# Log-sum-exp over heads on one core: 4 MB block loads, and an earlier, direct crossing from whole tiles to half tiles

## The chip, the cores and the metric

The kernel runs on one core of one Trainium2 chip. The time is the device time of one execution in microseconds (us), and the median of several is quoted. A profile of one execution of each kernel was taken as well; its span is 1.7 to 2.2 us shorter than the device time of the same execution.

Names of the engines in the profile: PE is the matrix engine (PEld its weight loads), DVE the vector engine, ACT the scalar engine, POOL the GpSimd engine, SP the engine that here only issues transfers.

## The reference

```python
B, S, D, H = 8, 2048, 2048, 8          # float32; x is 134.2 MB
x_heads = x.reshape(B, S, H, Dh).transpose(0, 2, 1, 3)     # Dh = 256
x_heads = x_heads + bias[None, :, None, :]
x_tiled = np.repeat(x_heads, 2, axis=2)
lse = log(sum(exp(x_tiled), axis=-1))  # the maximum is taken out and put back
```

For each row and each of its 8 heads, one number comes out: the logarithm of the sum of 256 exponentials of x plus bias. Every result is written twice. The work is a stream: each of 134.2 MB is read once, and only 1 MB is written.

## The kernel before

x is worked off as 64 tiles of 256 rows (2 MB, two rows for each of 128 partitions). All four engines share a tile: PE adds the bias to the first three heads, ACT takes exponentials, POOL adds the bias to the last four heads, DVE multiplies head 3 by the exponential of its bias and adds up. Near the end, tiles are worked off in smaller pieces, so that less is left to do when the last byte lands.

```python
K = 2
NBUF = 9
BULK = dict(pe=3, acc=1, g0=4, late=True, fold=0)
MIXED = dict(pe=1, acc=1, g0=4, late=False, fold=0)
PROMPT_F1 = dict(pe=2, acc=2, g0=8, late=False, fold=1)
...
STAGES = [                       # first tile of a stage, its pieces
    (0, (BULK,)),                # whole tiles
    (54, (MIXED,)),              # whole tiles, less for PE
    (57, (PROMPT_F1, PROMPT_F1)),# half tiles (1 MB), two pieces
    (62, (SINGLE_F1, SINGLE_F1)),
    (63, (PROMPT_F2, TRIPLE)),
]
...
    T_PROMPT = STAGES[1][0]      # 54
```

A stage with two entries cuts its tiles into two pieces, `k0 = 0` and `k0 = 1`. A piece starts with its column `c0 = 0`.

```python
    for t in range(T):
        ...
        for k0, k1, c0, c1 in pieces(t):
            m = modes_of(t)[k0]
            ...
            if c0 == 0:
                if next_units and not m["late"]:
                    bias_there = put_bias(*next_units.pop(0))   # PE: bias of the next unit
                if t > T_PROMPT and m["g0"] == H:
                    keep_warm()                                 # PE: 3 matmuls without use
                if m["g0"] < H:
                    add = g_add(m, t, k0, k1)                   # POOL
                if t < T - 1 or k0 == 0:
                    flush(for_pool)          # ACT and DVE part of the unit before
            if t == T_PROMPT and c0 == 0:    # the first factors
                spread(one_ps, V0, W0)                                     # PE
                nc.scalar.activation(out=one_ps, in_=one_ps, func=ACT.Exp) # ACT
            ...
            for_pool.append(pool_part)       # later: exponential, reduction, next load
```

A "unit" is a whole tile or a half tile, worked off as one. `for_pool` holds back what needs POOL's addition: the exponential and the reduction of a whole tile are put into the queues one unit later. The "factors" are the exponentials of the bias of heads 1 and 2; from the small pieces on, DVE multiplies by them. Up to there their place in PSUM, `one_ps`, belongs to the PE part of whole tiles, which is why they are made at the crossing between the stages.

The softmax here doesn't subtract the row's maximum and nothing guards it: scores larger than these inputs give would overflow.

## Time and profile before

| | before |
|---|---|
| time, median of 3 | 326.7 us |
| profiled span | 325.4 us |
| loads | 57 of 2 MB, 12 of 1 MB, then smaller ones |
| busy share of DVE, POOL, ACT, PE | 87%, 89%, 81%, 81% |
| DMA | full in nearly every slice |

The prediction below shows the rows that tell what bounds the kernel. In the order of time, columns are start (us from the span's start), duration, engine, line, operation, operands and, in brackets, the engine's idle time just before and what ended it. At the crossing of before (tiles 53 and 54), and for the second half of tile 62:

```profile
274.37 2.34 ACT L331 ACTIVATE xt<-xt 128x2560 f32<-128x2560 f32 x1 [0.70 <-POOL xt L325]
277.05 0.58 ACT L500 ACTIVATE one_ps<-one_ps 128x512 f32<-128x512 f32 x1 [0.35 <-PE one_ps L182]
...
314.65 1.70 ACT L331 ACTIVATE xt<-xt 128x1792 f32<-128x1792 f32 x1
```

The first row is the exponential of tile 53, which had been held back. The second makes the factors, once, after a wait of 0.35 us for PE. The third will serve as a marker and is called the marker row below: it is the last exponential before the last tile, and from its start to the end of the span 10.75 us pass.

In the order of time of SP, the store of the first seven batches stands behind the last of the loads, so its start tells when the last loads were issued (SP waits there for earlier loads, 49.5 us in 18 waits over the whole of before, so it keeps pace with the DMA):

```profile
315.36 0.72 SPq L425 DMA_DIRECT2D out_dram<-res  x1
```

### The profile page before, as it was taken

The page shows a single profiled execution, that of the slowest core. Times are in us where ns is not written, and L with a number is a line of the kernel's source. Part 1 is how long each engine was busy: PE and PEld are TensorE (multiplying, and loading weights), DVE is VectorE, ACT ScalarE, POOL GpSimd, SP SyncE. Part 2 cuts the span into 40 slices and gives each one's busy share as a digit, 9 for nine tenths or more (in the row PEclk, how much of TensorE's full clock was granted, in tenths as well). Part 3 has the DMA queues.
Part 4 walks back from the last instruction along what each step waited for, and adds up shares of the span by engine and source line. Part 5 has one row for each costly group of instructions (what it writes and reads, how often), then busy time and mean ns, then how long its engine had stood idle before and what let it go on. Part 6 is the DMA issues. An engine that isn't in the chain of part 4 may idle for free.

```text
span 325.4 us, 2350 instructions
## 1 busy us (share of the span) xinstructions
PE 263.2 (81%) x649; PEld 98.6 (30%) x649; DVE 284.0 (87%) x306; ACT 264.7 (81%) x425; POOL 290.7 (89%) x123
## 2 busy tenths in 40 slices
PE   5398999599888789779779788887877897399984
PEld 2033333233323223223223223323223332044442
DVE  1008999999999999998998899989899799999985
ACT  1139999499969878987887969698788778889995
POOL 7999999899999999999999999999999899958874
PEclk9999999899979987997997979798998989569999
DMA  7999999999999999999999999999999999999995
GB/s 293 428 435 429 427 433 422 425 433 429 427 427 431 425 424 433 425 425 434 426 425 431 431 422 427 429 429 427 431 427 426 429 425 429 415 421 421 424 394 154
DMA packets 11934, 135.42 MB, mean 416 GB/s; under 512 B 1361, under 2 KB 1745, under 8 KB 2961
## 3 DMA queue, kind: packets, MB, share of 16 engines
q1 hardware_dynamic: 11824, 135.27, 98.9%
q8 instruction: 5, 0.08, 0.1%
q14 instruction: 7, 0.06, 0.0%
q0 software_dynamic: 96, 0.00, 0.0%
q10 hardware_dynamic: 2, 0.01, 0.0%
HBM read 134.23 MB, written 1.05 MB: 416 GB/s over the span
## 4 chain that ended last, share of the span: by engine, by line
DMA 48%; DVE 35%; POOL 6%; ACT 6%; PE 3%; issue 1%; SPq 0%; DVEq 0%
DMA xt<-in_x_dram 45%; DVE R L350 29%; ACT xt L331 5%; DVE xt L343 5%; POOL xt L325 4%; DMA b<-bparts 2%; PE pair L275 2%; DVE xt L366 2%; PE one_ps L275 1%; ACT xt L293 1%; DMA brow<-in_bias_dram 1%; POOL brest L173 1%; POOL brest L175 1%; PE pair L216 0%; POOL bparts L172 0%
## 5 line engine op out<-in xcount | busy, mean ns | idle before, releaser
L325 POOL TENSOR_TENSOR xt<-xt,b_rep 128x2048 f32<-128x2048 f32 x57 | 258.8, 4543 | 20.1 <-DMA xt<-in_x_dram 20.1
L350 DVE TENSOR_REDUCE R<-xt 128x14 f32<-128x3584 f32 (+1 forms) x56 | 214.5, 3831 | 1.9
L331 ACT ACTIVATE xt<-xt 128x2560 f32<-128x2560 f32 (+5 forms) x77 | 158.1, 2062 | 13.4 <-POOL xt L325 12.5
L275 PE MATMUL pair<-xt,ident 128*128 128x512 f32 x216 | 115.1, 660 | 0.0
L275 PE MATMUL one_ps<-xt,ident 128*128 128x512 f32 x108 | 66.7, 702 | 23.1 <-DMA xt<-in_x_dram 23.1
L293 ACT ACTIVATE xt<-pair 128x1024 f32<-128x1024 f32 x54 | 56.3, 1042 | 20.7 <-PE pair L275 19.3
L275 PEld LDWEIGHTS pair<-xt,ident 128*128 128x128 f32 x216 | 46.2, 214 | 61.5 <-issue 61.5
L343 DVE TENSOR_TENSOR xt<-xt,w_ps 128x512 f32<-128x512 f32 x54 | 36.8, 681 | 27.8 <-ACT xt L331 27.7
L286 ACT ACTIVATE xt<-one_ps 128x256 f32<-128x256 f32 x108 | 40.6, 391 | 7.9 <-PE one_ps L275 7.9
L216 PE MATMUL one_ps<-b,ones 3*128 3x512 bf16 x54 | 20.7, 383 | 18.4 <-ACT xt L286 12.4
L216 PEld LDWEIGHTS <-ones 3*128 3x128 bf16 x162 | 13.5, 92 | 70.2 <-issue 63.8
L216 PE MATMUL pair<-b,ones 3*128 3x512 bf16 x108 | 32.3, 378 | 0.0
L275 PEld LDWEIGHTS one_ps<-xt,ident 128*128 128x128 f32 x108 | 17.0, 198 | 46.4 <-DMA xt<-in_x_dram 39.6
L251 PE MATMUL pair<-xt,ident 128*128 128x512 f32 (+1 forms) x36 | 21.0, 669 | 7.2 <-DMA xt<-in_x_dram 7.1
L286 ACT ACTIVATION_READ_ACCUMULATOR xt<-one_ps 128x1 f32 x108 | 23.5, 218 | 0.0
L366 DVE CUSTOM_DVE_ANT_0 xt<-xt,w_ps 128x256 f32<-128x256 f32 x61 | 22.4, 419 | 0.0
L390 POOL TENSOR_TENSOR xt<-xt 128x128 f32<-128x128 f32 (+3 forms) x39 | 13.9, 356 | 3.1
L382 POOL TENSOR_TENSOR xt<-xt,w_sb 128x256 f32<-128x256 f32 (+1 forms) x13 | 10.1, 773 | 5.4 <-ACT xt L331 4.8
L266 PE MATMUL tpair<-ident 128*128 128x128 f32 x84 | 13.6, 300 | 0.5 <-ACT res L421 0.5
L306 ACT ACTIVATE xt<-pair 128x256 f32<-128x256 f32 x33 | 12.3, 387 | 0.0
L266 PEld LDWEIGHTS tpair<-ident 128*128 128x128 f32 x84 | 11.1, 200 | 4.1 <-issue 3.0
L366 DVE CUSTOM_DVE_ANT_0 xt<-xt,one_ps 128x256 f32<-128x256 f32 x27 | 10.6, 416 | 0.7 <-ACT xt L331 0.7
(40 smaller groups left out, 68.5 us busy)
## 6 DMA issues: line engine op xcount, KB each, us to landing
xt<-in_x_dram SPq DMA_DIRECT2D x57, 2048.0 KB, 30.8
xt<-in_x_dram SPq DMA_DIRECT2D x12, 1024.0 KB, 24.7
xt<-in_x_dram SPq DMA_DIRECT2D x4, 256.0 KB, 11.4
out_dram<-res SPq DMA_DIRECT2D x1, 896.0 KB, 6.6
xt<-in_x_dram SPq DMA_DIRECT2D x2, 384.0 KB, 16.0
xt<-in_x_dram SPq DMA_DIRECT2D x2, 128.0 KB, 6.3
out_dram<-res_last SPq DMA_DIRECT2D x1, 128.0 KB, 1.7
b<-bparts POOLq DMA_DIRECT2D x3, 1.5 KB, 6.4
```

The costliest lines, as they stand in the source:

```text
L216: nc.tensor.matmul(p, lhsT=ones3, rhs=each_row(b3, h * Dh, Dh, K), start=True, stop=False,)
L251: mm = nc.tensor.matmul(p, lhsT=ident, rhs=xts[t % NBUF][:, ka:kb, c : c + w], start=False, stop=True,)
L266: nc.tensor.matmul(tps[B % 2][:, 0], lhsT=ident, rhs=ident, start=True, stop=True)
L275: mm = nc.tensor.matmul(p, lhsT=ident, rhs=xts[t % NBUF][:, :, h * Dh : (h + 1) * Dh], start=False, stop=True,)
L286: act = nc.scalar.activation(out=xts[t % NBUF][:, k, 0:Dh], in_=got[0][:, k * Dh : (k + 1) * Dh], func=ACT.Exp, accum_out=sums[:, k, 0:1],)
L293: act = nc.scalar.activation(out=xts[t % NBUF][:, :, Dh : m["pe"] * Dh].rearrange("p k (h j) -> p h k j", j=Dh), in_=got[-1].rearrange("p ...
L325: add = nc.gpsimd.tensor_tensor(out=v, in0=v, in1=each_row(b_rep, c - G0, D - c, k1 - k0), op=ALU.add)
L331: return on_x(t, nc.scalar.activation(out=v, in_=v, func=ACT.Exp), [after])
L343: mul = nc.vector.tensor_tensor(out=f, in0=f, in1=each_row(w_ps, m["pe"] * Dh - W0, n, k1 - k0), op=ALU.mult,)
L350: red = nc.vector.tensor_reduce(out=sums[:, k0:k1, h0:H], in_=v.rearrange("p k (h j) -> p k h j", j=Dh), op=ALU.add, axis=mybir.AxisListTy ...
L366: ttr = nc.vector.tensor_tensor_reduce(out=v, in0=v, in1=w, scale=1.0, scalar=0.0, op0=ALU.mult, op1=ALU.add, accum_out=dst,)
L390: done = nc.gpsimd.tensor_tensor(out=v[:, :, 0:n], in0=v[:, :, 0:n], in1=v[:, :, n : 2 * n], op=ALU.add)
```

## The change

The intent: larger loads have fewer packets (the profile counts 11934 in before) and fewer ends, so a kernel that waits for bytes gets them sooner. Tiles 2 to 49 are loaded in pairs of 4 MB, the buffers (8 instead of 9) are freed in pairs, the mixed stage goes, and half tiles begin at tile 52 instead of 57. Warm matmuls go into the bank that the next unit will fill, and other preparations move.

```diff
 K = 2
-NBUF = 9
+KB = 4
+BLOCKS = 50
+NBUF = 8
+NEARLY = 5
...
 STAGES = [
     (0, (BULK,)),
-    (54, (MIXED,)),
-    (57, (PROMPT_F1, PROMPT_F1)),
+    (52, (PROMPT_F1, PROMPT_F1)),
     (62, (SINGLE_F1, SINGLE_F1)),
...
     def load(t):
+        if TB <= t < BLOCKS:
+            if t % TB == 0:
+                ...                      # waits for the last uses of both tiles of the buffer
+                    nc.sync.dma_start(
+                        out=xbs[t // TB % len(xbs)], in_=rows_of(t, TB)
+                    ),
+                ...
+            return
...
+                for _ in range(NWARM):   # in put_bias, outside the whole tiles
+                    mm = nc.tensor.matmul(
+                        p[:, 0:P], lhsT=ident, rhs=ident, start=True, stop=True
+                    )
...
-                if t > T_PROMPT and m["g0"] == H:
-                    keep_warm()
                 if m["g0"] < H:
                     add = g_add(m, t, k0, k1)
-                if t < T - 1 or k0 == 0:
+                if t != T_PROMPT and (t < T - 1 or k0 == 0):
                     flush(for_pool)
             if t == T_PROMPT and c0 == 0:
-                spread(one_ps, V0, W0)
-                nc.scalar.activation(out=one_ps, in_=one_ps, func=ACT.Exp)
+                first_factors()
```

Cut: the bias of the first five units goes to PE in three parts directly, the small transfers of the bias are issued by ACT instead of POOL, the other factors are made at tile 32, the sums and the transposes of a batch are laid out for four rows of a partition, and loads are issued from a list of their own. `T_PROMPT` is still the first tile of the second stage, now 52.

More of the change, by code (lines that the diff above doesn't have):

```diff
@@ L16 @@
 K = 2
-NBUF = 9
+KB = 4
+BLOCKS = 50
+NBUF = 8
+NEARLY = 5
 NWARM = 3
 BULK = dict(pe=3, acc=1, g0=4, late=True, fold=0)
-MIXED = dict(pe=1, acc=1, g0=4, late=False, fold=0)
 PROMPT_F1 = dict(pe=2, acc=2, g0=8, late=False, fold=1)
@@ L60 @@
     H, Dh = bias.shape
-    assert D == H * Dh and S % (P * K) == 0
+    assert D == H * Dh and S % (P * KB) == 0
     NBLK = S // (P * K)
+    NB = S // (P * KB)
+    TB = KB // K
     T = B * NBLK
     T_PROMPT = STAGES[1][0]
+    T_FACTORS = T // 2
     CPE = BULK["pe"] * Dh
@@ L84 @@
     brest = sb.tile([1, 2, CPE], F32, name="brest")
-    R = [sb.tile([P, K, H, NBLK], F32, name=f"R{b}") for b in range(B - 1)]
+    R = [sb.tile([P, KB, H, NB], F32, name=f"R{b}") for b in range(B - 1)]
     R_last = sb.tile([P, H, NBLK, K], F32, name="R_last")
-    res = sb.tile([H * NBLK, B - 1, P, K, 2], F32, name="res")
+    res = sb.tile([H * NB, B - 1, P, KB, 2], F32, name="res")
     res_last = sb.tile([P, P, 2], F32, name="res_last")
-    xts = [sb.tile([P, K, D], F32, name=f"xt{i}") for i in range(NBUF)]
+    xbs = [sb.tile([P, KB, D], F32, name=f"xb{i}") for i in range(NBUF // TB)]
+    xts = [xb[:, k : k + K] for xb in xbs for k in range(0, KB, K)]
     w_ps = pp.tile([P, W2 - W0], F32, name="w_ps")
@@ L96 @@
     ps = [p[:, c : c + MM] for p in pairs for c in (0, MM)]
-    tpair = pp.tile([P, 2, K, P], F32, name="tpair")
-    tps = [tpair[:, i] for i in range(2)]
+    tp = pp.tile([P, KB, P], F32, name="tp")
     def modes_of(t):
@@ L108, in pieces, with rows_of @@
         return [(k, k + 1, c0, c1) for k in range(K) for c0, c1 in cols[k]]
-    def rows_of(t):
-        b, blk = divmod(t, NBLK)
-        v = x[b, blk * P * K : (blk + 1) * P * K, :]
+    def rows_of(t, n=1):
+        b, at = divmod(t, NBLK)
         if b < B - 1:
-            return v.rearrange("(p k) d -> p k d", k=K)
+            blk, i = divmod(at, TB)
+            v = x[b, blk * P * KB : (blk + 1) * P * KB, :]
+            return v.rearrange("(p k) d -> p k d", k=KB)[:, i * K : (i + n) * K]
+        v = x[b, at * P * K : (at + 1) * P * K, :]
         return v.rearrange("(k p) d -> p k d", k=K)
-    users = [[] for _ in range(T)]
+    users = [[] for _ in xbs]
     def on_x(t, ins, after):
-        known = [u for u in users[t] if u.ins.engine != ins.ins.engine]
-        for before in range(t % NBUF, t, NBUF):
-            known += users[before]
-        for u in known:
-            if u not in after:
+        buf = users[t // TB % len(xbs)]
+        for t_u, u in buf:
+            same = u.ins.engine == ins.ins.engine
+            if u not in after and (not same or t_u % NBUF == t % NBUF and t_u < t):
                 tc.declare_no_dep(
-                    ins.ins, u.ins, reason="waited for by those it waits for"
+                    ins.ins,
+                    u.ins,
+                    reason="another tile, or waited for by those it waits for",
                 )
-        users[t].append(ins)
+        buf.append((t, ins))
         return ins
@@ L138, in load @@
     def load(t):
+        if TB <= t < BLOCKS:
+            if t % TB == 0:
+                after = [u for i in range(TB) if t >= NBUF for u in last_uses[t + i - NBUF]]
+                ins = on_x(
+                    t,
+                    nc.sync.dma_start(
+                        out=xbs[t // TB % len(xbs)], in_=rows_of(t, TB)
+                    ),
+                    after,
+                )
+                for i in range(TB):
+                    loads[t + i, 0, 0] = ins
+            return
         after = last_uses[t - NBUF] if t >= NBUF else []
@@ L148, in load, with reload @@
             )
+    def reload(t):
+        n = t + NBUF
+        if n < BLOCKS:
+            if n % TB == TB - 1:
+                load(n - TB + 1)
+        elif n < T:
+            load(n)
     order = tc.manual_schedule()
@@ L177 @@
     for i in range(3):
-        nc.gpsimd.dma_start(out=b3[i : i + 1, :], in_=bparts[:, i])
+        nc.scalar.dma_start(out=b3[i : i + 1, :], in_=bparts[:, i])
     def spread(dst, c0, c1):
@@ L188, with first_factors, other_factors @@
         nc.vector.tensor_copy(b_rep[:, c - G0 : c - G0 + MM], ps[i])
-    for c in range(W0, W2, MM):
-        spread(w_ps[:, c - W0 : c - W0 + MM], c, c + MM)
-    nc.scalar.activation(out=w_ps, in_=w_ps, func=ACT.Exp)
-    nc.scalar.activation(out=w_sb, in_=b_rep[:, W1 - G0 :], func=ACT.Exp)
+    w_late = w_ps[:, 0 : G0 - W0]
+    spread(w_late, W0, G0)
+    nc.scalar.activation(out=w_late, in_=w_late, func=ACT.Exp)
+    def first_factors():
+        spread(one_ps, V0, W0)
+        nc.scalar.activation(out=one_ps, in_=one_ps, func=ACT.Exp)
+    def other_factors():
+        nc.scalar.activation(
+            out=w_ps[:, G0 - W0 :], in_=b_rep[:, 0 : W2 - G0], func=ACT.Exp
+        )
+        nc.scalar.activation(out=w_sb, in_=b_rep[:, W1 - G0 :], func=ACT.Exp)
     n_ps = [0]
@@ L214, in put_bias @@
             got = [one_ps, pair[:, 0:MM], pair[:, MM : 2 * MM]]
+            parts = [(ones3, b3)]
+            if n_ps[0] <= NEARLY:
+                parts = [(ones3[0:1], bparts[:, i]) for i in range(3)]
             for h, p in enumerate(got):
-                nc.tensor.matmul(
-                    p,
-                    lhsT=ones3,
-                    rhs=each_row(b3, h * Dh, Dh, K),
-                    start=True,
-                    stop=False,
-                )
+                for i, (lhsT, b) in enumerate(parts):
+                    nc.tensor.matmul(
+                        p,
+                        lhsT=lhsT,
+                        rhs=each_row(b, h * Dh, Dh, K),
+                        start=i == 0,
+                        stop=False,
+                    )
             return got + [pair]
@@ L232, in put_bias @@
                 n_ps[0] += 1
+                for _ in range(NWARM):
+                    mm = nc.tensor.matmul(
+                        p[:, 0:P], lhsT=ident, rhs=ident, start=True, stop=True
+                    )
+                    on_bank(bank, mm)
                 mm = nc.tensor.matmul(
@@ L262, in add_x @@
         return heads
-    def keep_warm():
-        for _ in range(NWARM):
-            nc.tensor.matmul(
-                tps[B % 2][:, 0], lhsT=ident, rhs=ident, start=True, stop=True
-            )
     def late_heads(m, t, got, sums):
@@ L401, in add_up @@
             )
-            on_x(t, red, [done])
+            last_uses[t].append(on_x(t, red, [done]))
         return add_up
     def finish(b):
-        nr = H * NBLK
-        tp = tps[b % 2]
-        for k in range(K):
+        nr = H * NB
+        for k in range(KB):
             nc.tensor.transpose(
@@ L418, in finish @@
             offset=tp.offset,
-            ap=[[tp.ap[0][0], nr], [1, P], [P, K], [0, 2]],
+            ap=[[tp.ap[0][0], nr], [1, P], [P, KB], [0, 2]],
         )
@@ L425, in store @@
         nc.sync.dma_start(
-            out=out[0 : B - 1].rearrange("b h (n r) -> (h n) b r", n=NBLK),
+            out=out[0 : B - 1].rearrange("b h (n r) -> (h n) b r", n=NB),
             in_=res.rearrange("q b p k r -> q b (p k r)"),
@@ L430, in finish_last @@
     def finish_last():
-        tp = tps[(B - 1) % 2][:, 0]
+        last = tp[:, KB - 1]
         nc.tensor.transpose(
-            out=tp, in_=R_last.rearrange("p h n k -> p (h n k)"), identity=ident
+            out=last, in_=R_last.rearrange("p h n k -> p (h n k)"), identity=ident
         )
         tv = bass.AP(
-            tensor=tp.tensor, offset=tp.offset, ap=[tp.ap[0], [1, P], [0, 2]]
+            tensor=last.tensor, offset=last.offset, ap=[last.ap[0], [1, P], [0, 2]]
         )
@@ L448, in sums_of @@
         if b < B - 1:
-            return R[b][:, :, :, blk]
+            return R[b][:, blk % TB * K :, :, blk // TB]
         return R_last[:, :, blk, :].rearrange("p h k -> p k h")
@@ L455 @@
     for_pe = []
+    for_load = []
     next_units = [
@@ L471 @@
     for t in range(T):
+        if t == T_FACTORS:
+            other_factors()
         xt = xts[t % NBUF]
@@ L511 @@
                 flush(for_pe)
+                flush(for_load)
             if not m["late"]:
@@ L525, in pool_part @@
                     later(m, t, k0, k1, sums, add)
-                if k1 == K and t + NBUF < T:
-                    load(t + NBUF)
+                if k1 == K:
+                    for_load.append(lambda: reload(t))
             for_pool.append(pool_part)
```

## The prediction

> **What bounds the kernel now.** I read the page's 40 slices first, then busy time by stretch, then the DMA view in two windows, then single engines in order of time.
>
> From the page:
>
> ```profile
> DMA  7999999999999999999999999999999999999995
> GB/s 293 428 435 429 427 433 422 425 433 429 427 427 431 425 424 433 425 425 434 426 425 431 431 422 427 429 429 427 431 427 426 429 425 429 415 421 421 424 394 154
> ```
>
> The 16 DMA engines are full from the second slice to the one before the last. Every compute engine has more idle time than that (DVE 87%, POOL 89%, ACT 81% busy). So in the bulk the kernel waits for bytes: its time is the start before the first packet, the time that the packets need, and what is left to do after the last one. The chain of waits agrees with 45% on the loads; where it names DVE, from 26 to 121 us, DVE works off a late start with full buffers behind it and the DMA is as full as later.
>
> Busy time by stretch (columns: window, length, busy time per engine, clock, DMA share, GB/s):
>
> ```profile
> 180.00:260.00 80.00, 65.92 (x152) 23.30 (x151) 74.02 (x34) 67.02 (x103) 73.36 (x18) 0.91 1.01 428
> 280.00:290.00 10.00, 7.65 (x11) 1.75 (x11) 10.00 (x28) 8.54 (x13) 8.68 (x2) 0.50 1.01 422
> 290.00:300.00 10.00, 9.51 (x45) 5.50 (x45) 10.00 (x49) 10.00 (x19) 6.56 (x15) 0.96 1.01 420
> ```
>
> Full in all three, but 428 GB/s with 2 MB loads and 420 with 1 MB loads. The DMA view of a window of each kind shows what differs (230 to 260 us, then 290 to 310 us):
>
> ```profile
> DMA packets 879, 12.82 MB, mean 427 GB/s; under 512 B 96, under 2 KB 96, under 8 KB 96
> ...
> q8 instruction: 1, 0.02, 0.2%
> q14 instruction: 1, 0.01, 0.1%
> ```
>
> ```profile
> DMA packets 1156, 8.41 MB, mean 421 GB/s; under 512 B 129, under 2 KB 129, under 8 KB 129
> ```
>
> Without the tiny ones: 783 packets for 12.82 MB, 16.4 KB each, which is two 8 KB rows, what one partition gets from a 2 MB load. In the later window 1027 packets for 8.41 MB, 8.2 KB, one row. The tiny ones are some 16 to a load. So each engine moves 8 large packets and a tiny one per load, and the large one is as long as the contiguous run of a partition.
>
> The price of a packet comes from arrivals. POOL's addition starts when its tile has landed (it waited about 0.35 us for the DMA each time), and so does PE in the half units:
>
> ```profile
> 185.90 4.54 POOL L325 TENSOR_TENSOR xt<-xt,b_rep 128x2048 f32<-128x2048 f32 x1 [0.34 <-DMA xt<-in_x_dram]
> ...
> 249.54 4.55 POOL L325 TENSOR_TENSOR xt<-xt,b_rep 128x2048 f32<-128x2048 f32 x1 [0.35 <-DMA xt<-in_x_dram]
> 255.10 4.54 POOL L325 TENSOR_TENSOR xt<-xt,b_rep 128x2048 f32<-128x2048 f32 x1 [1.02 <-DMA xt<-in_x_dram]
> ...
> 279.59 4.55 POOL L325 TENSOR_TENSOR xt<-xt,b_rep 128x2048 f32<-128x2048 f32 x1 [0.38 <-DMA xt<-in_x_dram]
> 284.55 4.54 POOL L325 TENSOR_TENSOR xt<-xt,b_rep 128x2048 f32<-128x2048 f32 x1 [0.41 <-DMA xt<-in_x_dram]
> ```
>
> ```profile
> 304.64 1.13 PE L251 MATMUL pair<-xt,ident 128*128 128x512 f32 x2 [0.19 <-DMA xt<-in_x_dram]
> ...
> 312.11 0.70 PE L251 MATMUL pair<-xt,ident 128*128 128x256 f32 x2 [0.29 <-DMA xt<-in_x_dram]
> ```
>
> 185.90 to 249.54 is 13 tiles, 4.895 us each. 304.64 to 312.11 is three 1 MB loads, 2.49 each, 4.98 for 2 MB: 0.085 us more, for 8 more large packets and one more tiny packet per engine. The tile that lands at 284.55 (the first of the last batch, whose two rows of a partition lie apart, so 16 packets but one load) took 4.96, 0.065 more. So about 8 ns a large packet and some 20 ns for the end of a load. Take the 0.085 off 4.895 and 2 MB costs 4.81 us, 436 GB/s. The step of 5.56 at 255.10 is 0.67 us above its neighbours; the window holds two instruction fetches[...].
>
> [...] here the granted clock falls to 0.50 in 280 to 290 us, where PE has few matmuls.
>
> **The change part by part.**
>
> Block loads. Tiles 2 to 49 come as 24 loads of 4 MB instead of 48 of 2 MB; a partition's run becomes 32 KB. Per pair an engine saves 8 large packets and one tiny one: 0.085 us. 24 x 0.085 = 2.0 us off the DMA's time, all of it on the path, since the DMA has no gap.
>
> Half units from tile 52 on instead of 57. Tiles 52 to 55 now arrive as halves with 8 KB runs: 4 x 0.085 = 0.34 us more; tile 56 had 8 KB runs already, 0.02 more. Net on the DMA: 2.0 - 0.36 = 1.7 us less.
>
> Eight tile buffers instead of nine, freed in pairs. When a block lands, POOL adds its two tiles in 2 x 4.55 = 9.1 us, then ACT 2.34, DVE 0.60 and 3.89: the buffer is free some 16 us after landing. The other three blocks keep the DMA fed for 3 x 9.7 = 29 us. [...] The DMA doesn't run dry. POOL has 9.1 of work per 9.7, DVE 2 x 4.52 = 9.0, ACT 2 x 4.0 = 8.0: all below it.
>
> The start. The bias parts go to PE directly for five units and don't wait for the small transfers (7.1 us in the chain). DVE starts perhaps 6 to 8 us earlier. The DMA was full anyway: 0 us, but it keeps the smaller buffer safe, since eight tiles last only to about 42 us.
>
> Warm matmuls into the next bank, factors later, four transposes per batch and 32-partition logarithms (0.58 us becomes perhaps 1.0): off the path, 0 us, except in the catching up below.
>
> The crossing to half units. Let L be the landing of tile 51. Its block neighbours landed at L - 9.8, so POOL's additions of 48 to 51 end at L - 5.2, - 0.7, + 3.9, + 8.4 (before, the last bulk addition ended 4.6 after landing). ACT: exponential of 50 from 3.9 to 6.1, PE part of 51 to 7.9, factors to 8.4, first half unit to 9.8, exponential of 51 to 12.0, second half unit and heads to 14.1. From there each half costs ACT 2.09 us:
>
> ```profile
> 301.14 1.50 ACT L331 ACTIVATE xt<-xt 128x1536 f32<-128x1536 f32 x1
> ...
> 303.23 1.51 ACT L331 ACTIVATE xt<-xt 128x1536 f32<-128x1536 f32 x1
> ```
>
> and 2.49 of DMA. The second half of tile 62 is 19 halves later: 14.1 + 19 x 2.09 + 1.0 for a logarithm = 54.8; it lands at 22 x 2.49 = 54.8. So ACT has just caught up where the end begins (before, it had by 309.6 us). DVE needs 1.80 a half and follows ACT. The sum is exact only to about 1 us, and a lag there goes straight onto the end: I add 0.3 us as its mean.
>
> Sum: 326.7 - 1.7 + 0.3 = 325.3 us.
>
> **The rivals.**
>
> A, packets stay at 16 KB or the 32 KB run gains nothing: 24 saved load ends at 0.02 are 0.5 us, less 0.36 for the halves. Time 326.6. Against it: 8 to 16 KB pays as computed. I give it 15%.
>
> B, the crossing is too abrupt and ACT is still behind at tile 62: the end moves by up to 1.5 us, time 325.5 to 326.8. For it: the 3.9 us that POOL is later. Against it: five more tiles in which to gain 0.4 us a half. 25%.
>
> C, buffers freed in pairs let the DMA run dry: each gap would show as a slice below 9. [...] 3%, time above 328.
>
> D, [...] 1% of the rate would cost 2 to 3 us and eat the gain. 5%.
>
> E, the earlier start or the shorter crossing saves more than counted. [...]
>
> **Range and chances.** Mostly the sum holds: 324.6 to 325.8. Rivals A and B reach 326.8, a better packet price 324.2. Range 324.2 to 326.7. A gain of over 2% needs 320.2; without any fixed part 134.2 MB at 436 GB/s take 308 us, plus about 2.5 before and 7.5 after, some 318, so 24 merged pairs cannot give it: 1%. Slower by 2% needs a starved DMA: 1%. Within 2%: 98%.
>
> **What would show each step.** In a bulk window 32.8 KB per large packet and 431 to 432 GB/s instead of 428; pairs landing every 9.7 us; DMA at 9 in every slice of the bulk. Half units at 420 GB/s from about 260 us on. POOL waiting less than 1 us between blocks, clock near 0.9 or more in the crossing. DVE's first reduction near 19 us, without effect on the total. ACT waiting for the DMA again at tile 62. The prediction is wrong if large packets stay at 16.4 KB, if SP's waits leave DMA slices below 9, or if the stretch from the last landing to the end grows by more than 1 us.

The sum came to 326.7 - 1.7 + 0.3 = 325.3 us. The 1.7 us are 24 x 0.085 = 2.0 for the pairs less 0.36 for the halves. The 0.085 us a pair, like the 8 ns a large packet and the 20 ns for the end of a load, is the author's estimate from the measured steps of 4.895, 4.98 and 4.96 us; that a run of 32 KB stays one packet was an assumption. For the buffers the numbers are 29 us of loads against 16 us until a buffer is free.

## The result, and the profile after

| | before | after |
|---|---|---|
| time, median (range, executions) | 326.9 us (326.6 to 327.1, 4) | 331.55 us (330.3 to 332.2, 4) |
| profiled span | 325.4 us | 329.9 us |
| mean granted clock of PE | 0.921 | 0.917 |

The ratio is 1.014, with a 95% interval of 1.011 to 1.017. Ratios here are the mean time of one kernel's fast runs over the mean of the other's in the same rounds, so they are not quite the ratio of the medians that are quoted. The time is longer by about 4.6 us, where 1.4 us less had been predicted. All outputs are right.

The DMA did as foreseen. The page of after:

```profile
DMA  8999999999999999999999999999999999999960
GB/s 313 447 441 429 413 435 438 441 425 421 437 437 439 421 418 441 437 433 418 429 437 436 433 417 437 433 441 421 429 419 421 419 421 420 424 415 424 408 236 16
```

Full up to two slices before the end, then 60% and nothing: the bytes came sooner, and the last 8 us went by with the DMA almost idle. In the row of before, in the prediction, the last slice still carries 154 GB/s. The rate is around 430 GB/s in the bulk and 420 with half tiles. The DMA view of 100 to 200 us, and POOL in order of time (two of its starts, 11 pairs apart):

```profile
DMA packets 1478, 42.98 MB, mean 430 GB/s; under 512 B 163, under 2 KB 163, under 8 KB 163
```

```profile
62.81 9.04 POOL L373 TENSOR_TENSOR xb<-xb,b_rep 128x2048 f32<-128x2048 f32 x2 [0.65 <-DMA xb<-in_x_dram]
...
169.69 9.06 POOL L373 TENSOR_TENSOR xb<-xb,b_rep 128x2048 f32<-128x2048 f32 x2 [0.71 <-DMA xb<-in_x_dram]
```

Without the tiny ones, 1315 packets carried 42.98 MB: 32.7 KB each. 106.88 us for 11 pairs is 9.716 us a pair, against 2 x 4.895 before: 0.074 us less. (9.716 us for 4 MB are 432 GB/s.) And SP comes to its store 2.3 us sooner than in before:

```profile
313.08 0.35 SPq L472 DMA_DIRECT2D out_dram<-res  x1
```

The landings agree: the load of the second half of tile 62 landed at 314.6 us in before (issued at 294.5, 20.1 us to landing) and at 312.4 in after (292.5 and 19.9). The last of all loads landed 5.6 us before the end of the span in before and 11.5 us before it in after. The prediction had named growth of this stretch by more than 1 us as a sign of being wrong.

What is late is ACT. ACT in order of time at the crossing (tiles 51 and 52), and for the second half of tile 62:

```profile
266.00 1.02 ACT L341 ACTIVATE xb<-pair 128x1024 f32<-128x1024 f32 x1 [1.48 <-PE pair L323]
269.88 0.58 ACT L230 ACTIVATE one_ps<-one_ps 128x512 f32<-128x512 f32 x1 [2.86 <-PE one_ps L217]
270.38 1.48 ACT L379 ACTIVATE xb<-xb 128x1536 f32<-128x1536 f32 x1
273.53 0.58 ACT L230 ACTIVATE one_ps<-one_ps 128x512 f32<-128x512 f32 x1 [1.67 <-PE one_ps L217]
274.02 1.48 ACT L379 ACTIVATE xb<-xb 128x1536 f32<-128x1536 f32 x1
...
276.11 3.71 ACT L379 ACTIVATE xb<-xb 128x2560 f32<-128x2560 f32 x2
...
319.08 1.68 ACT L379 ACTIVATE xb<-xb 128x1792 f32<-128x1792 f32 x1
```

In the bulk a wait of ACT cost nothing: data then collected in the buffers, and ACT was faster than they came (in after it was busy for 84.6 us of the stretch from 100 to 200 us, with the DMA full). Here it has too little time left to catch up. Three waits for PE stand in 9 us, where the two rows of before show 0.70 us for POOL and 0.35 us for PE: 1.48 us for PE's matmuls of tile 51, 2.86 us for the factors, and 1.67 us for the factors **again**: the operation that writes `one_ps` is there twice. The exponential of tile 51 comes only at 276.11 (the first of the two in that row), though its data are ready from 265.7 us on, when the last of POOL's four additions ends:

```profile
247.65 18.03 POOL L373 TENSOR_TENSOR xb<-xb,b_rep 128x2048 f32<-128x2048 f32 x4 [0.69 <-DMA xb<-in_x_dram]
```

The last row of ACT is the marker row: 319.08 instead of 314.65, 4.43 us later. The span is 4.5 us longer. What follows this row is as long as before (10.8 us), so the whole loss arises before it.

The same stretch on PE, in order of time:

```profile
261.45 2.07 PE L323 MATMUL one_ps<-xb,ident 128*128 128x512 f32 x2
263.32 2.64 PE L323 MATMUL pair<-xb,ident 128*128 128x512 f32 x4
...
268.83 1.02 PE L217 MATMUL one_ps<-brow,ones 1*128 1x512 f32 x2
...
272.37 1.12 PE L217 MATMUL one_ps<-brow,ones 1*128 1x512 f32 x2 [0.48 <-DVE R L414]
```

The six matmuls of tile 51 took 4.7 us; a tile of before took 1.12 + 1.88 us near its own crossing. Such slow tiles are not special to after: in before the six matmuls from 259.97 us on took 4.5 us, and ACT waited for them too:

```profile
264.55 1.02 ACT L293 ACTIVATE xt<-pair 128x1024 f32<-128x1024 f32 x1 [1.71 <-PE pair L275]
```

The granted clock in 260 to 265 us was 0.66 in both traces.

Then, in after, between 265.8 and 268.8, PE does the warm matmuls and the bias of the next units and the first half tile, all ahead of the factors. It makes them a second time at 272.37, after waiting 0.48 us for DVE, which was still reading the first ones.

How much of that is lag? In the prediction's plan for ACT, the list "exponential of 50" to "second half unit and heads" ends 14.1 us after tile 51 lands, at about 271.6 us. In the trace the same list, with the exponential of tile 51 last, ends at 276.11 + 2.34 = 278.45: 6.8 us later. The plan had ACT catch up with the data exactly at tile 62. The data for the second half of tile 62 landed at about 312.3 us (314.65 - 2.3, and by the landing above), ACT took them up at 319.08, again 6.8 us. So the balance is -2.3 from the DMA and +6.8 from ACT, together +4.5.

### The profile page after: what moved, and what is told of

It reads as the page before. It is cut to its first block, busy times and chain, and to the rows that moved or that the text cites. A ratio compares the mean times of both kernels' runs of the same rounds, so it can differ in the third digit from the quotient of the medians.

```text
span 329.9 us, 2665 instructions
## 1 busy us (share of the span) xinstructions
PE 280.7 (85%) x762; PEld 114.1 (35%) x762; DVE 281.1 (85%) x373; ACT 267.4 (81%) x447; POOL 282.8 (86%) x155
## 2 busy tenths in 40 slices
DMA packets 8849, 135.46 MB, mean 411 GB/s; under 512 B 1057, under 2 KB 1441, under 8 KB 2433
## 4 chain that ended last, share of the span: by engine, by line
DMA 26%; ACT 25%; DVE 23%; PE 22%; POOL 3%; issue 0%; SPq 0%; DVEq 0%
DMA xb<-in_x_dram 25%; DVE R L398 18%; ACT xb L379 16%; PE pair L323 9%; PE one_ps L323 5%; ACT xb L354 4%; PE pair L265 3%; DVE xb L391 3%; POOL xb L373 3%; PE one_ps L265 2%; DVE xb L414 2%; ACT xb L341 2%; PE pair L217 1%; ACT xb L334 1%; ACT res L468 1%; DMA brow<-in_bias_dram 1%
## 5 line engine op out<-in xcount | busy, mean ns | idle before, releaser
L373 POOL TENSOR_TENSOR xb<-xb,b_rep 128x2048 f32<-128x2048 f32 x52 | 235.1, 4543 | 21.6 <-DMA xb<-in_x_dram 21.6
L398 DVE TENSOR_REDUCE R<-xb 128x14 f32<-128x3584 f32 x52 | 202.2, 3888 | 1.8
L379 ACT ACTIVATE xb<-xb 128x2560 f32<-128x2560 f32 (+5 forms) x79 | 158.2, 2008 | 9.1 <-POOL xb L373 9.1
L323 PE MATMUL pair<-xb,ident 128*128 128x512 f32 x208 | 113.6, 674 | 0.0
L323 PE MATMUL one_ps<-xb,ident 128*128 128x512 f32 x104 | 66.4, 724 | 11.1 <-DMA xb<-in_x_dram 11.1
L341 ACT ACTIVATE xb<-pair 128x1024 f32<-128x1024 f32 x52 | 53.7, 1032 | 26.4 <-PE pair L323 26.4
L323 PEld LDWEIGHTS pair<-xb,ident 128*128 128x128 f32 x208 | 45.9, 221 | 61.5 <-issue 61.5
L391 DVE TENSOR_TENSOR xb<-xb,w_ps 128x512 f32<-128x512 f32 x52 | 35.4, 681 | 29.6 <-ACT xb L379 29.5
L334 ACT ACTIVATE xb<-one_ps 128x256 f32<-128x256 f32 x104 | 38.6, 383 | 6.7 <-PE one_ps L323 6.6
L414 DVE CUSTOM_DVE_ANT_0 xb<-xb,w_ps 128x256 f32<-128x256 f32 x95 | 34.2, 416 | 0.0
L323 PEld LDWEIGHTS one_ps<-xb,ident 128*128 128x128 f32 x104 | 16.6, 201 | 32.7 <-DMA xb<-in_x_dram 16.8
```

Source lines behind the costliest of these rows:

```text
L323: mm = nc.tensor.matmul(p, lhsT=ident, rhs=xts[t % NBUF][:, :, h * Dh : (h + 1) * Dh], start=False, stop=True,)
L334: act = nc.scalar.activation(out=xts[t % NBUF][:, k, 0:Dh], in_=got[0][:, k * Dh : (k + 1) * Dh], func=ACT.Exp, accum_out=sums[:, k, 0:1],)
L341: act = nc.scalar.activation(out=xts[t % NBUF][:, :, Dh : m["pe"] * Dh].rearrange("p k (h j) -> p h k j", j=Dh), in_=got[-1].rearrange("p ...
L373: add = nc.gpsimd.tensor_tensor(out=v, in0=v, in1=each_row(b_rep, c - G0, D - c, k1 - k0), op=ALU.add)
L379: return on_x(t, nc.scalar.activation(out=v, in_=v, func=ACT.Exp), [after])
L391: mul = nc.vector.tensor_tensor(out=f, in0=f, in1=each_row(w_ps, m["pe"] * Dh - W0, n, k1 - k0), op=ALU.mult,)
```

## The experiments

Theory **F**: the factors are made twice, because the condition `t == T_PROMPT and c0 == 0` holds for both pieces of tile 52; that and their late place in PE's queue cost most of the lag. Theory **S**: the crossing itself, without the mixed stage, is too abrupt. Theory **P**: pairs that land just before the crossing leave POOL, and then ACT, behind. Later came **O**: the flush that after skips at the crossing is what fills ACT's wait in before, and **W**: PE's slow clock at the crossing. (The first expectations call F theory T, and S and P together rival R.) The runs were made in four groups, each on one chip with before beside it (326.76 to 326.89 us median).

| run | what | median us (range, executions) | ratio to before, 95% interval |
|---|---|---|---|
| e1_once | factors once | 328.28 (327.7-330.0, 6) | 1.0054 (1.003-1.007) |
| e2_once_early | once, before tile 52 | 327.36 (325.9-328.6, 6) | 1.0019 (1.000-1.004) |
| e3_blocks_old_stages | after, stages of before | 331.0 (329.8-332.3, 6) | 1.0130 (1.011-1.015) |
| e4_thrice | factors three times | 331.62 (330.8-334.0, 6) | 1.0172 (1.014-1.020) |
| e5_no_blocks | after, 2 MB loads | 330.36 (329.2-330.5, 5) | 1.0103 (1.009-1.012) |
| e6_early_blocks40 | e2, pairs to tile 39 | 326.35 (326.1-329.1, 6) | 1.0017 (0.999-1.005) |
| e7_early_cross48 | e2, halves from 48 | 326.63 (326.6-326.7, 5) | 0.9996 (0.998-1.001) |
| e8_old_stages_blocks40 | e3, pairs to tile 39 | 327.38 (327.2-329.2, 6) | 1.0027 (1.001-1.004) |
| e9_cross50 | e2, halves from 50 | 326.23 (326.1-326.3, 5) | 0.9983 (0.997-1.000) |
| e10_early_warm | e2, warm matmuls earlier | 327.15 (327.0-328.7, 6) | 1.0025 (1.001-1.004) |
| e11_no_blocks_early | e2, 2 MB loads | 327.68 (327.4-330.6, 6) | 1.0054 (1.002-1.008) |
| e12_cross50_warm | e9 with e10 | 326.26 (326.0-326.3, 5) | 0.9982 (0.997-1.000) |
| e13_flush | after, flush not skipped | 331.7 (331.0-332.8, 5) | 1.0145 (1.013-1.016) |
| e14_flush_once | e1, flush not skipped | 327.32 (325.6-328.5, 6) | 1.0010 (0.999-1.004) |
| e15_old_stages40_flush | e8, flush not skipped | 325.17 (325.1-326.7, 6) | 0.9955 (0.994-0.997) |
| e16_old_stages50_flush | e3, flush not skipped | 327.82 (327.1-329.4, 6) | 1.0035 (1.002-1.005) |

Differences between two runs below are taken from their ratios, times 326.8 us, unless medians are named.

### e1_once and e2_once_early: the factors made once, and where

```diff
-            if t == T_PROMPT and c0 == 0:
+            if t == T_PROMPT and k0 == 0:        # e1
                 first_factors()
```

```diff
-            if t == T_PROMPT and c0 == 0:        # e2: not here,
-                first_factors()
...
                 if m["late"]:
+                    if t == T_PROMPT - 1:        # but right after the PE part of tile 51
+                        first_factors()
                     bias_there = put_bias(*next_units.pop(0))
```

> Kernel after, with the exponential of the early bias factors made once, at the first half of tile 52, not again at its second half. Theory T (the second making of the factors and the wait for the first hold ACT up in the crossing, and the delay goes straight to the end, because ACT gains only 0.4 us a half unit): ACT loses 1.67 us of idle and 0.50 of work less, so about 2.1 us faster than after: 329.3 to 329.6 us. Rival R (the crossing is too abrupt: pairs make POOL late, five tiles more of half units, whatever is done with the factors): within 0.5 us of after, 331 to 332.

> Kernel after, with the factors made once and right after the last bulk tile's PE part, ahead of the next unit's warm and bias matmuls on PE. Theory T: both idle stretches of ACT (2.86 and 1.67 us) and the second exponential (0.5) go, ACT starts the half units about 5 us earlier: 326 to 327 us, with ACT still some 1.5 us behind at tile 62. Rival R: within 1 us of after, 330.5 to 332.

Against after's 1.0139, making them once is worth 2.8 us, and making them early as well 3.9 us. ACT of e2 in order of time, where the two rows follow each other without a wait:

```profile
268.09 0.58 ACT L230 ACTIVATE one_ps<-one_ps 128x512 f32<-128x512 f32 x1
268.58 2.85 ACT L379 ACTIVATE xb<-xb 128x1536 f32<-128x1536 f32 x2
```

Both waits for the factors are gone and two half tiles go through at once. This is most of what after had lost, but not all: e2 is still no faster than before, although its DMA is. In its profile the marker row stands at 315.01, 2.8 us after its data landed (312.2).

### e4_thrice: the suspected cost doubled

```diff
-            if t == T_PROMPT and c0 == 0:
+            if (t == T_PROMPT or t == T_PROMPT + 1 and k0 == 0) and c0 == 0:
                 first_factors()
```

> Kernel after, with a third making of the factors at the first half of tile 53: the suspected cost once more. Theory T: one more idle stretch of ACT of the same kind, 1.5 to 2.2 us slower than after: 333 to 333.8 us. Rival R: within 0.5 us of after.

Measured: 1.1 us more than after by the ratios, with intervals that overlap (1.011 to 1.017, and 1.014 to 1.020), and nothing by the medians; two of the six runs took 334 us. The expected cost was not reached. The profile, of one of the shorter runs (330.83 us), shows the third making without a wait, because the held-back exponential of tile 51 runs just ahead of it:

```profile
274.89 2.34 ACT L379 ACTIVATE xb<-xb 128x2560 f32<-128x2560 f32 x1
277.12 0.60 ACT L230 ACTIVATE one_ps<-one_ps 128x512 f32<-128x512 f32 x1
```

There it costs its own 0.5 us on ACT. This suggests that a making costs what ACT waits for it, not a fixed sum: whether there is other work ahead of it in the queue decides. That is what led to theory O.

### e3_blocks_old_stages and e8_old_stages_blocks40: the blocks with the stages of before

```diff
+MIXED = dict(pe=1, acc=1, g0=4, late=False, fold=0)
...
-    (52, (PROMPT_F1, PROMPT_F1)),
+    (54, (MIXED,)),
+    (57, (PROMPT_F1, PROMPT_F1)),
```

e8 has `BLOCKS = 40` as well, so that the last pair is 38 and 39.

> Kernel after, with the stages of before: bulk to tile 53, three mixed tiles 54 to 56, half units from 57 on; block loads, start, warm matmuls as in after. The factors are then made once, since the first crossing tile is one piece. Theory T: ACT has caught up by the end, the DMA's gain remains: 326.9 - 2 = 324.5 to 325.3 us. If the blocks themselves make the crossing late (a part of rival R: pairs leave POOL 4 us behind), ACT is behind at the end and the time is 327 or more.

> The kernel with the stages of before and blocks (331.0 us, where I had expected 325), with blocks only to tile 39. Theory P: POOL is level with the DMA again at the crossing, the lag there goes, and with it most of the wait for the factors: 325.5 to 327 us. If the stages of before fail with this kernel for another reason (the warm matmuls in the next bank, the delayed flush), it stays at 330 us or more.

Theory S alone would have e3 at or below before. It is as slow as after. In the mixed stage a tile is a single piece, so the factors are made once; yet ACT's order of time in e3 shows one wait as long as after's two together:

```profile
278.99 0.58 ACT L232 ACTIVATE one_ps<-one_ps 128x512 f32<-128x512 f32 x1 [4.31 <-PE one_ps L219]
```

e8 has this wait as well, 4.31 us, and still is 3.4 us faster than e3. What differs is POOL: in e3 it works without a pause from 247.58 on (nine additions in 40.54 us), still late from the last pair when the crossing comes, while in e8 it has caught up by 258 us and again waits 0.35 us for each tile. So P is a part of it, and S alone is not what makes after slow. A direct comparison is e1 with e3: both have pairs up to tile 49, the factors once and the flush skipped, and differ in the stages. e1, with the crossing of after, is 2.5 us faster. The 4.31 us were new and fell outside what had been expected.

### e5_no_blocks and e11_no_blocks_early: the crossing without the blocks

```diff
-BLOCKS = 50
+BLOCKS = 2       # every tile a load of 2 MB; e5 from after, e11 from e2
```

> Kernel after with no block loads at all: every whole tile is a 2 MB load again, the rest (the factors made twice, the crossing at 52) as in after. Theory P (pairs that land together leave POOL, ACT and DVE some 4 to 5 us behind at the crossing, on top of the waits for the factors): the DMA needs 2.3 us more, but ACT enters the half units about 5 us earlier relative to the data, so 328 to 329.5 us, faster than after although its DMA is slower. Theory F (only the factors delay the crossing, the blocks are a pure gain): 331.5 + 2.3 = 333.5 to 334 us.

> The kernel with the factors once and early without any block loads (crossing at 52). Against 327.4 us with blocks to 49. Theory P: the DMA needs 2.1 us more, ACT's lag is 3 us less and so nothing is left of it: 326.8 to 327.5 us, the same within the noise: the blocks' gain on the DMA and their cost at the crossing cancel. If the blocks cost nothing at the crossing: 329 us or more.

e5 is 1.2 us faster than after, though it takes its bytes more slowly. Its marker row stands at 317.88, 3.8 us behind its data (landed at 314.1), where after has 6.8. So about 3 of after's 6.8 us come from the pairs, which is the slack that the prediction had spent on POOL being 3.9 us late; the other part is there without any pair, and ACT's waits for the factors are the same 2.86 and 1.67 us. P missed by 0.9 us here and F by 3.1. With the factors made early e11 is 0.3 us slower than e2 by the medians and 1.1 us by the ratios, with intervals that overlap (two of its six runs are 3 us longer than the other four): about the same, as expected for P. In e11 ACT waits for data again near the end (its marker row at 314.90), while e2 takes its bytes sooner and is 2.8 us behind them.

### e6_early_blocks40: fewer pairs, the early factors

```diff
-BLOCKS = 50
+BLOCKS = 40      # on top of e2
```

> The kernel with the factors made once and early (327.4 us), with blocks only up to tile 39, then twelve 2 MB loads before the crossing, in which POOL gains 0.35 us a tile on the DMA, 4.2 us in all. Theory P: the rest of ACT's lag at tile 62 (2.7 us) goes, five blocks fewer cost the DMA 0.5 us: 325 to 325.8 us. Theory F: 327.4 + 0.5, 327.5 to 328.5 us.

Four runs lie between 326.1 and 326.4 us, two at 329. By its ratio e6 does not differ from e2, by the median it is 1.0 us faster. The four have a mean granted clock of 0.937 to 0.947, the two 0.926. That a lower clock of PE in the crossing makes the spread is the author's guess: only one run of each kernel was profiled, and what differs from one execution to the next is not shown by any run.

### e7_early_cross48 and e9_cross50: half tiles from earlier on

```diff
-BLOCKS = 50
+BLOCKS = 46
...
-    (52, (PROMPT_F1, PROMPT_F1)),
+    (48, (PROMPT_F1, PROMPT_F1)),      # e7; e9 has 50; both on top of e2
```

> The kernel with the factors made once and early (327.4 us), with the crossing at tile 48 instead of 52 and blocks to 45, so that two 2 MB loads stand before it as before. Eight more half units in which ACT gains 0.4 us each, 3.2 us, against 2.7 us of lag; the DMA pays 0.085 x 4 + 0.09 x 2 = 0.5 us. If the end is set by a lag that half units work off: 325.2 to 326 us. If half units bring costs of their own that I have not seen (rival R): 327.5 us or more.

> Factors once and early, crossing at tile 50, blocks to tile 45, so four 2 MB loads before the crossing: four half units more than in the 327.4 us kernel (1.6 us of ACT's lag worked off) and two more single loads for POOL (0.7 us), for 0.3 us of DMA. If the end is set by ACT's lag: 325.3 to 326.3 us, level with or a little under the crossing at 48 (326.6 us). If four half units aren't enough: 326.8 us or more.

If the crossing were too abrupt (S), an earlier one gives ACT more half tiles to catch up in, 0.4 us each (2.49 us of DMA less 2.09 of ACT). It does: the marker row stands at 313.58 in e7 and 313.62 in e9, the half before it waits 0.3 us for the DMA, and all runs lie within 0.2 us (e2: 2.7 us). They are bound by bytes up to there, as before is. The edit also ends the pairs earlier, so by itself it does not tell S from P. What is left is small, since each tile in halves gives back 0.085 us of DMA time (4.98 us for two loads of 1 MB, 4.895 for one of 2 MB) and fewer pairs save it: e9 ends 0.17% below before, as expected, and e7 0.6 us above what was expected of it. In e7 11.2 us pass from the marker row to the end, instead of 10.8; why is not shown.

### e10_early_warm and e12_cross50_warm: PE's clock at the crossing

```diff
             got = [one_ps, pair[:, 0:MM], pair[:, MM : 2 * MM]]
+            if n_ps[0] > 42:             # the last whole tiles
+                for _ in range(NWARM):
+                    nc.tensor.matmul(
+                        got[1][:, 0:P], lhsT=ident, rhs=ident, start=True, stop=True
+                    )
```

e10 is e2 with this, e12 is e9 with this.

> The kernel with the factors once and early (327.4 us, its runs from 325.9 to 328.6), with three warm matmuls also ahead of the bias of each bulk tile from 42 on, put in the time that PE waits for ACT to empty its bank. Theory W ([...] the matmuls of tile 51 take 4.6 us instead of 2.8 and ACT idles 1.5 us for them; whether it happens in a run makes the spread): 325.5 to 326.3 us, spread under 1 us. If the clock doesn't matter: 327 to 328 us with the same spread, or more for PE's added work.

> Crossing at 50, blocks to 45, factors once and early, and the warm matmuls before the crossing: everything that should take the lag away. Theories T, P and W together: only the DMA bounds it, 324.8 to 325.8 us, 0.3 to 0.6 percent under the kernel before, spread under 1 us. If instruction fetches or the end take back more than I count: 326 us or more.

In after, PE waited 1.46 us before the bias of tile 51, with a granted clock of 1.00 from 259 to 261 us; in 262 to 264 us, in the matmuls of tile 51, it was 0.50. The wait of 1.5 us for these matmuls is gone from e10, and its marker row waits for the DMA (313.30). The total does not move, against expectation: now PE is slow after that, and ACT waits 0.49 and 0.93 us for it in the last tile. The second of the two rows:

```profile
320.79 0.38 ACT L359 ACTIVATE xb<-pair 128x256 f32<-128x256 f32 x1 [0.93 <-PE pair L310]
```

By stretch, PE's granted clock in 300 to 325 us is 0.92 in e10, against 0.98 in e2 and 1.00 in after, e9 and e12; in 260 to 300 us it is 1.00 in e10 and in e12. e12 has the time of e9, 0.5 us above the upper end of what was expected, though it has the same added matmuls as e10 and kept its clock. (Of the instruction fetches that its expectation names, the page of before counts 12 packets, 0.14 MB, 0.1% of the DMA engines' time; what took the 0.5 us is not shown.) So W names a real wait, but no run turned it into time, and what moves the slow stretches about is not shown.

### e13_flush and e14_flush_once: the order of before at the crossing

```diff
-                if t != T_PROMPT and (t < T - 1 or k0 == 0):
+                if t < T - 1 or k0 == 0:           # e13 from after, e14 from e1
                     flush(for_pool)
```

> Kernel after with one thing undone: the exponential of the last bulk tile is issued ahead of the factors again, as before, instead of being put off until both halves of tile 52 are through. Theory O (the order: ACT waits 2.86 us for the first making of the factors with nothing in its queue, and that exponential, 2.3 us and ready, would fill the wait): about 2.2 us off after: 329 to 329.6 us. If the first wait doesn't matter (only the second making does): 331 to 332 us.

> Kernel after with the order of before (last bulk exponential ahead of the factors) and the factors made once. Theories O and T: 2.2 and 2.2 to 2.8 us off after, so level with the kernel with the factors once and early: 326.8 to 327.6 us. If O is wrong: 328.3 us, as with the factors once alone.

With this line the exponential of tile 51 stands ahead of the factors again. Alone it changes nothing (331.7 us). ACT in order of time shows why:

```profile
271.55 0.58 ACT L230 ACTIVATE one_ps<-one_ps 128x512 f32<-128x512 f32 x1 [0.64 <-PE one_ps L217]
...
277.10 0.58 ACT L230 ACTIVATE one_ps<-one_ps 128x512 f32<-128x512 f32 x1 [3.58 <-PE one_ps L217]
```

The first wait shrinks from 2.86 to 0.64 us, as theory O has it. But now DVE adds up tile 51 first, reads the first factors later, and PE waits 2.39 us for it before it may write the second ones; ACT's second wait grows from 1.67 to 3.58 us. The two faults lean on each other. With the factors made once (e14), the order of before is worth 1.4 us beyond e1. ACT of e14 in order of time:

```profile
265.80 2.34 ACT L379 ACTIVATE xb<-xb 128x2560 f32<-128x2560 f32 x1 [0.33 <-POOL xb L373]
268.27 0.58 ACT L230 ACTIVATE one_ps<-one_ps 128x512 f32<-128x512 f32 x1
...
313.16 1.70 ACT L379 ACTIVATE xb<-xb 128x1792 f32<-128x1792 f32 x1
...
320.65 0.38 ACT L354 ACTIVATE xb<-pair 128x256 f32<-128x256 f32 x1 [1.53 <-PE pair L305]
```

With the pairs up to tile 49 and the crossing at 52, as in after, no wait for the factors is left. ACT was free for the marker row at 313.05 us, only 0.7 us after 312.3, where after has 6.8; in this run the data came at 313.1. So the plan of the prediction holds to within 1 us once the factors are made once and in the order of before. What this run lost, it lost later: 1.53 us for PE in the last tile; the mean granted clock of the profiled run was 0.932.

### e15_old_stages40_flush and e16_old_stages50_flush: the blocks alone, with the crossing of before

```diff
-                if t != T_PROMPT and (t < T - 1 or k0 == 0):
+                if t < T - 1 or k0 == 0:           # e15 from e8, e16 from e3
                     flush(for_pool)
```

> The stages of before, blocks to tile 39 (327.4 us, where its profile has ACT idle 4.31 us for the factors) with the order of before. Theory O: the exponential of tile 53 fills 2.2 us of the 4.31 us wait, the lag of some 1.2 us at tile 62 goes, the DMA bounds the end: 325.5 to 326.3 us. If O is wrong: 327 to 327.6 us.

> The stages of before with blocks to tile 49 (331.0 us, my worst miss) with the order of before. Theory O: 2.2 us less, 328.5 to 329.2 us, and what is left over before is the lateness of the pairs. If the pairs alone made that lag: 330.5 to 331.5 us.

The line is worth 3.1 us in e16 (against e3) and 2.3 us in e15 (against e8). This settles why e3 and e8 had missed: they had the stages of before, but not its order. ACT of e15 in order of time:

```profile
272.35 2.34 ACT L381 ACTIVATE xb<-xb 128x2560 f32<-128x2560 f32 x1 [0.70 <-POOL xb L375]
275.96 0.58 ACT L232 ACTIVATE one_ps<-one_ps 128x512 f32<-128x512 f32 x1 [1.27 <-PE one_ps L219]
...
312.30 1.70 ACT L381 ACTIVATE xb<-xb 128x1792 f32<-128x1792 f32 x1
```

The exponential of tile 53 fills the wait for the factors, of which 1.27 us stay. The marker row stands at 312.30, 2.35 us before that of before: the whole gain of the DMA arrives there and in the span, which is 2.4 us shorter. e15 takes 325.17 us, 0.45% (1.5 us) less than before, and is the fastest version here; it beats both kernels. In the profiled run 0.4 us more than in before lies outside the span; why is not shown. e15 has the 8 buffers, the new start, the warm matmuls and the new layout of after, so none of these makes after slow. One of its six runs, with the lowest clock (0.913), took 326.7. e16, with pairs up to tile 49, is 2.6 us slower: its additions run back to back through the crossing as in e3, and its marker row stands at 314.00, 2.0 us behind its data. Both came out faster than expected. e14 differs from e16 in the stages alone and is 0.8 us faster, so here too the new crossing itself is not what costs time: S falls as the cause.

## Why the prediction was right or wrong

**What bounds the kernel, and the block loads: right.** The packets became 32.7 KB, a pair saves 0.074 us (0.085 predicted), so 24 pairs save 1.8 us (2.0 predicted), and the DMA had no gap. Loads queued one behind the other from SP ran at about 420 GB/s with 1 MB (2.49 us each), 428 with 2 MB (4.895 us each) and 432 with 4 MB (9.716 us a pair). Rivals A, C and D fell with that. The loads were through 2.3 us sooner, net, where 1.7 was predicted. By the pairs and the halves it would be 1.8 - 0.36 = 1.4 us. Some 0.35 us of the rest can be estimated from the first slice (313 GB/s instead of 293 over 8 us is about 0.15 MB); 0.5 us were not taken apart. e5 gives the split another way: without any pair the second half of tile 62 lands at 314.1 us, so the pairs are worth 1.7 us of the 2.3 and the rest of the change, halves included, 0.5. Of the two instruction fetches that the prediction names beside a load 0.67 us late, one ran at 255.9 us, after that load had landed (POOL began on it at 255.10), and two fetches at 187.6 and 188.8 us delayed no addition of POOL (it waited 0.35 us for the DMA at 190.79, as elsewhere); what made that load late is not shown.

**The start: no effect on the time, as said.** DVE's first reduction came at 21.0 us instead of 26.6 (19 predicted). That the bytes themselves would start a little sooner, rival E, had been counted at 0 us.

**The step that failed is "The crossing to half units", and in the sum the term "+ 0.3".** It measured 6.8 us. The step itself was sound in what it said of POOL: the exponential of tile 50 was planned 3.9 us after tile 51 landed (261.4 us) and began at 261.48. It was also sound in its warning that "a lag there goes straight onto the end". What it lacked was every wait between ACT and PE. It took PE as done whenever ACT came, and the factors as 0.5 us. Measured: 1.48 us for the matmuls of tile 51, 2.86 us for the first making, 1.67 us and another 0.5 us for a second making that the diff contains and I did not see. That makes 6.5 of 6.8; 0.3 us are longer durations or unread. Three parts have their runs: the second making with e1 (2.8 us together with the wait for DVE that it brings), its place with e2 (1.1 us more), the skipped flush with e14, e15 and e16 (1.4 to 3.1 us). These do not add up one by one, since the parts lean on each other (e13). The 1.48 us for the matmuls are read from the trace alone: where they went (e10), the time did not move, and before has such waits too.

**Rival B had the right name and the wrong size.** It allowed "up to 1.5 us" at 25%, because the plan let ACT catch up just in time. With pairs up to tile 49 that plan had no slack left: e5 has 3 us less lag than after with the same waits. But the crossing was not too abrupt in itself (e14 against e16, e1 against e3). A plan without slack has no symmetrical error, since ACT can only be late.

**"Warm matmuls, factors later ...: off the path, 0 us, except in the catching up below": the exception was priced at 0.5 us for the factors and at nothing for the warm matmuls.** Three warm matmuls stand ahead of each bias in PE's queue just where ACT waits for PE, two such groups of 0.8 us ahead of the first making in after; no run takes out the warm matmuls alone. The logarithm was 1.0 us long as foreseen (0.59 in before).

**The skipped flush was in the diff and was not priced.** In the trace ACT kept to the order of its queue: the exponential of tile 51 was ready at 265.7 us, stood behind waits of 2.86 and 1.67 us, and began at 276.11. Had I asked of each moved line what then stands behind a wait, this would have shown.

**What the forecast got for the wrong kernel:** 325.3 us had been predicted, and e15, which has fewer pairs and no new crossing, takes 325.2. For 19 pairs and no more halves the prediction's own price would give 1.6 us, 325.1; that the forecast for the other kernel meets e15's number is chance. The DMA's gain was at least what it was said to be; the change as made hid it. What stays open is the spread of about 3 us in runs of the same kernel (e2, e4, e6, e11, e14). In e6, e10, e11 and e14 the longer runs have the lower mean granted clock, in e4 they do not; the cause no run shows. Open is also whether the clock at the crossing can be raised without paying for it later.

## What to carry to other kernels

When a stage boundary moves, ask how often each action tied to it now runs: a condition that held once for a whole tile holds twice when the first tile of the stage is cut in two. ACT kept to the order of its queue here (work that was ready at 265.7 us began at 276.11, behind two waits), so put work that is ready ahead of a wait for another engine, and read a removed flush as a moved queue. The 4 MB loads handed over data in lumps (POOL had two additions, 9.04 us, to do at each landing, and ACT was 6.8 us behind its data near the end, against 3.8 without pairs): give the consumer some small loads to catch up on before a stage in which it has no slack, and price the waits between the engines there, not only their work.
